# A two-layer fp32 encoder on one core: value weights loaded in layer 1's last phase, own buffers for raw weights, the last gated outputs kept on chip

## The chip, the cores and the metric

The kernel runs on one core of one Trainium2 chip. The metric is the device time of one execution in microseconds (us); the median of three runs of the kernel before is 2820.6 us (2820.55 to 2821.27). Engines are named as in the profile: PE is the matrix engine, PEld its loading of the stationary operand, DVE the vector engine, ACT the scalar engine, POOL GpSimd, and SP the engine whose queue issues all DMAs here, in one fixed order.

## The reference

The input x has 2048 tokens of 1024 channels. Layer 1 is a gated MLP mixer, layer 2 banded attention over the present and the eight previous chunks of 64 tokens, with 16 heads of 64 channels, a relative bias and a SiLU gate. Keys and values are projected from the residual stream after layer 1.

```python
h = rms_norm(x, a_norm_g);  x = x + gmlp_mixer(h, ...)         # layer 1
k, v = split(rms_norm(x, g_kv) @ w_kv)                         # shared keys, values
q, z = split(rms_norm(x, b_norm_g) @ w_qz)                     # layer 2
o = softmax(q * scale @ k.T + bias, band of 9 chunks) @ v      # per head
x = x + (o * silu(z)) @ w_out
return rms_norm(x, final_norm_g)
```

All of it is float32. The kernel writes every float32 product as three matmuls of a high and a low half (`mm3`, L111): high by high, high by low, low by high. Each operand is therefore split first: ACT casts the high half (L190, L226, L257) and DVE subtracts it to get the low half (L191, L227, L258).

## The kernel before

Tokens are worked in four tiles of 512 (t = 0 to 3), heads in eight pairs (p = 0 to 7). A scheduler at build time reorders the instructions of each engine by readiness; the order of the program text, the sizes of the buffer rings and the waits of rings for their last readers bound what it can do. A ring is a tag with `bufs` places: a new tile must wait until the readers of the tile that had its place are done.

The stages, by their time in the profiled execution:

- **Layer 1**, 0 to 1346.9. Its last part is the output product `Po`, a Strassen product of seven phases from 1037.9 on. Beside it `v_sums` prepares the value weights of the seven phases and stores them in DRAM (`vwf`). `block(0, b)` transposes the normed x of tile 0 and splits it at once into `hh`/`hl`, the two halves of the transposed x (16 KB per partition each).
- **Value stage** `vp`, 1346.9 to 1538.5. Per tile 14 products (seven phases in the order 1, 7, 2, 6, 5, 4, 3, two column halves `jp`), each of 12 matmuls. In tile 0 `v_right` loads the weights of each phase from `vwf` into `st` (2 places) as it is reached, and splits them. The loop also norms and transposes the x of tile t+1: all four `norm` calls stand at the tile's start, the four `block` calls at its steps 20, 28, 36 and 44.
- **Attention**, tile by tile from 1538.5, 1838, 2150 and 2465. For each pair `ahead` yields, in small steps, the products of the next pair: q and k (`project`), the gate z (`gate`), each 24 matmuls (`pj`), and a share of the Strassen out product `bo` of the tile before (`SHARE`, 56 steps per tile). The pair loop takes these steps between the eight scores `s`, transposes of the probabilities `tp` (`flip`) and value products `pv` of the present pair; `per` 16 spreads them over all eight rounds.
- **Weights of `pj`** (`weights`, L189): a raw weight of 512 KB is loaded on SP (L198 for t > 0, L200 for t = 0, where POOL also scales it by a gain at L181 and it is stored again), cast by ACT (`wh_b`, L190) and reduced by DVE (`wl_b`, L191). Raw, high and low half all take places of the one ring `T` of 8, which `bo`'s weights use too (loaded in halves from `ows`, L219).
- **`o_sums`** (L1213): makes the Strassen sums of the out weights in four units, each of four loads, seven splits, four POOL operations and 14 stores to `ows`. They run in pairs 1 to 4 of tile 0.
- **Gated outputs** `og` (L1366): stored per pair to DRAM (`ogd`) and loaded again as the quarters `A` by `o_left`, with sums on POOL (L1393).
- **Tail**, 2752.5 to 2808.5: `bo` of tile 3, which has no attention beside it.
- **`finish`** (L1448 to L1461): the final norm of a finished block: for t < 3 the row `y` is loaded back from DRAM (ring `bx`, 2 places), scaled and stored.

Of the kernel before, what the change touches and what calls it, by code (L numbers as in the profile page):

```python
# [33 lines left out]
def trunk_kernel(  # L34
# [34 lines left out]
    }  # L69
    khd = [  # L70
# [74 lines left out]
    th0 = []  # L145

    def block(t, b):
# [8 lines left out]
        if t == 0 and b == 0:  # L156
            th0.extend(x_tiles(0))
        for h in range(2):
            ks = slice(h * 4, h * 4 + 4)
            nc.scalar.copy(x3[:, ks, :], half[h][:])  # L160
            if t == 0:
                oh = th0[0][:, ks, b * P : (b + 1) * P]
                nc.scalar.copy(oh, half[h][:])
                tv(th0[1][:, ks, b * P : (b + 1) * P], half[h][:], oh.bitcast(F32), op=sub)
        if t > 0:
            nc.sync.dma_start(xtd[t][b][:], xt[:])
# [19 lines left out]
    def t_tile(name):  # L186
        return sh.tile([P, 1024], F32, tag="T", name=name, bufs=8)
# [5 lines left out]
    def weights(t, p, c):  # L193
        name = f"b{t}_{p}_{c}"
        raw = t_tile(f"raw_{name}")
# [10 lines left out]
    def o_right(t):  # L206
        def right(ph):
            out = []
            for q in range(2):
                name = f"bo{t}_{ph}_{q}"  # L210
                if t + 1 == NT and ph in (2, 3):
                    raw = t_tile(f"raw_{name}")
                    w = [w_tile(f"w{i}_{name}") for i in "hl"]
                    nc.sync.dma_start(raw[:], wb_out[1, ph - 2, q])
# [8 lines left out]

    PHS = (1, 7, 2, 6, 5, 4, 3)

    def strassen(name, right, left, evict):  # L226
# [3 lines left out]

        def ready(i):
            if i < len(todo):
                ph, jp = todo[i]
                if jp == 0:
                    rts[ph] = right(ph)
                views[i] = left(ph, jp)

        ready(0)
        for i, (ph, jp) in enumerate(todo):
            ps = pmm.tile([P, 512], F32, tag="mm", name=f"{name}_{ph}_{jp}")  # L240
            vs = views.pop(i)
            for k in range(4):
                hi, lo = rts[ph][k // 2]
                c = slice((k % 2) * 512, (k % 2) * 512 + 512)
                mm3(ps[:], *vs[k], hi[:, c], lo[:, c], k == 0, k == 3)
                if k == 1:
                    ready(i + 1)
                if k < 3:
                    yield
# [3 lines left out]
    def split_s(pool, bufs, name, src):  # L253
# [5 lines left out]
        return [(hi[:, k, :], lo[:, k, :]) for k in range(4)]  # L259

    with ExitStack() as actx:
# [732 lines left out]
        for u in range(4):  # L994
            for f_, o in zip(v_sums(u), (0, 4, 5, 7, 9)):
                at(nin + 6 + 11 * u + o, f_)
# [11 lines left out]

        at(nin + 51, b_open)
# [19 lines left out]
    with ExitStack() as vctx:  # L1029
        vp = vctx.enter_context(tc.tile_pool(name="vp", bufs=1, reuse_waits="tile"))  # L1030
        vw = {
            (ph, q): [vp.tile([P, 1024], F32R, name=f"vw{i}{ph}_{q}") for i in "hl"]
            for ph in (1, 7, 5, 4, 3) for q in range(2)
        }

        def v_right(t):
            def right(ph):
                if t == 0:
                    for q in range(2):
                        if ph in (2, 6):  # L1040
                            vw[ph, q] = [w_tile(f"vw{i}{ph}_{q}") for i in "hl"]
                        raw = vp.tile([P, 1024], F32, tag="st", name=f"st{ph}_{q}", bufs=2)
# [5 lines left out]
        def v_left(t):  # L1048
# [3 lines left out]
            def left(ph, jp):  # L1052
                a11, a12, a21, a22 = (raw(jp, r, h) for r in range(2) for h in range(2))
                quad = {1: (0, 0), 2: (0, 1), 4: (1, 1)}.get(ph)
                if t == 0 and quad:
                    r, h = quad
                    c = slice((2 * jp + r) * P, (2 * jp + r + 1) * P)
                    out = [(a[:, c], b[:, c]) for a, b in xT[t][4 * h : 4 * h + 4]]
                else:
                    src = {1: a11, 7: a11, 2: a12, 6: a11, 5: a21, 4: a22, 3: a12}[ph]  # L1060
                    out = split_s(
                        vp, 6, f"v{t}_{ph}_{jp}", src.rearrange("p (k c) -> p k c", k=4)
                    )
# [61 lines left out]
        for t in range(NT):  # L1125
            if t + 1 < NT:
                for b in range(TB):
                    norm(t + 1, b, v_junk)
            for i, _ in enumerate(strassen(f"vp{t}", v_right(t), v_left(t), v_evict(t))):
                if t + 1 < NT and i in (20, 28, 36, 44):  # L1130
                    block(t + 1, (i - 20) // 8)
        pt4x.close()
        ptr.open(name="ptr", bufs=1, space=PSUM)

    with ExitStack() as bctx:
        cb = bctx.enter_context(tc.tile_pool(name="cb", bufs=1, reuse_waits="tile"))
        sb = bctx.enter_context(tc.tile_pool(name="sb", bufs=2, reuse_waits="tile"))
        pss = bctx.enter_context(tc.tile_pool(name="bss", bufs=1, space=PSUM))
# [74 lines left out]

        def o_sums(u):

            q, i = divmod(u, 2)
            cs = slice(i * 512, i * 512 + 512)
            w = {}
            for rc in ((0, 0), (0, 1), (1, 1), (1, 0)):
                w[rc] = c_tile(f"wo{u}_{rc[0]}{rc[1]}")  # L1220
                nc.sync.dma_start(w[rc][:], wb_out[rc[0], rc[1], q][:, cs])
            b11, b12, b21, b22 = (w[k][:] for k in ((0, 0), (0, 1), (1, 0), (1, 1)))

            def keep(ph, src):
                hi, lo = (half_tile("S", f"so{u}_{ph}{x_}", 6, F32R) for x_ in "hl")
                nc.scalar.copy(hi[:], src)
                tv(lo[:], src, hi[:].bitcast(F32), op=sub)
                for n, y_ in enumerate((hi, lo)):
                    nc.sync.dma_start(ows[ph, q][:, n, cs], y_[:].bitcast(F32))

            def first():
                keep(1, b11)
                tg(b11, b12, b11, op=sub)
                tg(b12, b22, b12, op=sub)

            def second():
                keep(3, b22)
                tg(b22, b22, b11, op=sub)

            def third():  # L1240
                keep(2, b21)
                tg(b21, b21, b22, op=sub)

# [398 lines left out]
```

## Time and profile before

| what | value |
|---|---|
| median of three runs | 2820.6 us |
| profiled execution | 2819.17 us, of it 2817.4 us span |
| PE busy in the span | 2673.3 us, 95% |
| DVE, ACT, POOL busy | 1955.1, 1322.6, 907.6 us |
| loads and stores | 732.42 MB, mean 260 GB/s |
| stages: `Po`; value; attention t = 0, 1, 2, 3; tail | 309.0; 191.6; 299.5, 312.0, 315.0, 287.5; 56.0 us |

Two numbers are to be read together: how long PE had nothing in it (length of a stretch less PE's busy time), and PEclk, the clock that the throttle granted while it worked, as a share of full speed. At full speed a 128x512 matmul starts every 0.227 us, in slow stretches every 0.427 us. A row "PE pj L114 <- DVE wl_b L191: 11.2, 20, 1.2" says that PE's matmul `pj` of line 114 waited 11.2 us in 20 waits, 1.2 us at the longest, and that what ended the waits was DVE's `wl_b` of line 191.

### The profile page before, as it was taken

To read this page: it belongs to the slowest core of one execution; us is meant where nothing else is said; L and a number is where in the kernel's file an instruction comes from. 1 tells how busy PE (TensorE), PEld (TensorE's weight loads), DVE (VectorE), ACT (ScalarE), POOL (GpSimd) and SP (SyncE) were. 2 spreads that over 40 slices of the span, in tenths; PEclk is the share of its full clock that TensorE was granted. 3 is DMA by queue.
4 is the path that set the end of the run, shared out by engine and by line. 5 is a ranking of instruction groups with operands and counts; after the bars stand their busy time and mean duration, and the time that the engine had idled before them with its cause. 6 is when DMAs were issued, how large, how long until landed. Compare 5 with 4: busy or idle time off the path is not lost. (4 is left out here: it accounts for less than half of the span.)

```text
span 2817.4 us, 38771 instructions
## 1 busy us (share of the span) xinstructions
PE 2673.3 (95%) x13216; PEld 2220.0 (79%) x13216; DVE 1955.1 (69%) x3091; ACT 1322.6 (47%) x2356; POOL 907.6 (32%) x903
## 2 busy tenths in 40 slices
PE   8999999999999999999799878999989999999997
PEld 7888888888888888888578656788778887788775
DVE  5665776667666777567577565777777777877775
ACT  5422243434434343433554544655555555565552
POOL 3512244251532322041243444323232222322234
PEclk9999999999999999999999898999999999999997
DMA  7898999989989689685646777666667665765676
GB/s 299 322 335 322 365 336 333 327 316 332 322 292 326 246 302 344 210 286 210 231 171 218 250 258 255 207 206 199 207 212 252 206 207 184 262 206 180 193 231 242
DMA packets 274421, 732.42 MB, mean 260 GB/s; under 512 B 29488, under 2 KB 62256, under 8 KB 274224
## 3 DMA queue, kind: packets, MB, share of 16 engines
q1 hardware_dynamic: 274224, 729.94, 75.0%
q8 instruction: 105, 1.72, 0.2%
q14 instruction: 92, 0.75, 0.1%
HBM read 540.03 MB, written 179.31 MB: 255 GB/s over the span
## 5 line engine op out<-in xcount | busy, mean ns | idle before, releaser
L112 PE MATMUL P<-T,S 128*128 128x512 f32 x1248 | 495.7, 397 | 2.1 <-ACT S L311 2.1
L114 PE MATMUL P<-T,S 128*128 128x512 f32 x1248 | 489.8, 392 | 0.0
L113 PE MATMUL P<-T,S 128*128 128x512 f32 x1248 | 488.4, 391 | 1.1 <-DVE T L314 1.1
L1299 POOL TENSOR_SCALAR pr<-pr,sl 128x640 f32<-128x640 f32 (+4 forms) x256 | 206.1, 806 | 603.0 <-DVE sl L1298 529.8
L112 PE MATMUL pj<-hh_b,wh_b 128*128 128x512 f32 x768 | 318.3, 414 | 20.9 <-ACT wh_b L190 20.2
L114 PE MATMUL pj<-hh_b,wl_b 128*128 128x512 f32 x768 | 312.6, 407 | 14.2 <-DVE wl_b L191 13.9
L113 PE MATMUL pj<-hl_b,wh_b 128*128 128x512 f32 x768 | 307.8, 401 | 0.0
L114 PEld LDWEIGHTS P<-T,S 128*128 128x128 f32 x1248 | 234.9, 188 | 50.5
L112 PEld LDWEIGHTS P<-T,S 128*128 128x128 f32 x1248 | 235.5, 189 | 47.0 <-ACT S L311 2.3
L113 PEld LDWEIGHTS P<-T,S 128*128 128x128 f32 x1248 | 235.4, 189 | 46.7 <-DVE T L314 1.3
L1295 ACT ACTIVATE pr<-pr,nm 128x640 f32<-128x640 f32 (+4 forms) x256 | 195.0, 762 | 147.9 <-DVE nm L1288 147.0
L1323 DVE TENSOR_TENSOR pt<-tp,pt 128x640 fp32r<-128x640 f32 (+4 forms) x256 | 188.3, 736 | 61.5 <-ACT pt L1322 59.8
L1288 DVE CUSTOM_DVE_ANT_0 pr<-s,bias 128x640 f32<-128x640 f32 (+4 forms) x256 | 188.4, 736 | 50.4 <-PE s L1280 40.8
L1319 PE MATMUL tp<-ident,pr 128*128 128x128 f32 x1120 | 168.7, 276 | 33.7 <-DVE pt L1323 29.1
L1319 PEld LDWEIGHTS tp<-ident,pr 128*128 128x128 f32 x1120 | 133.8, 141 | 77.2 <-issue 32.2
L114 PEld LDWEIGHTS pj<-hh_b,wl_b 128*128 128x128 f32 x768 | 148.3, 193 | 56.4 <-DVE wl_b L191 25.5
L1322 ACT CAST pt<-tp 128x640 fp32r<-128x640 f32 (+4 forms) x256 | 158.2, 618 | 68.5 <-PE tp L1319 66.1
L112 PEld LDWEIGHTS pj<-hh_b,wh_b 128*128 128x128 f32 x768 | 148.7, 194 | 47.5 <-ACT wh_b L190 26.2
L113 PEld LDWEIGHTS pj<-hl_b,wh_b 128*128 128x128 f32 x768 | 148.9, 194 | 18.9
L191 DVE TENSOR_TENSOR wl_b<-raw_b,wh_b 128x1024 fp32r<-128x1024 f32 x96 | 130.7, 1361 | 46.1 <-ACT wh_b L190 40.1
L1347 PE MATMUL pv<-pt,V 128*128 128x256 f32 x960 | 152.2, 294 | 2.0 <-ACT pt L1322 2.0
L190 ACT CAST wh_b<-raw_b 128x1024 fp32r<-128x1024 f32 x96 | 100.7, 1049 | 111.1 <-DMA raw_b<-wk 57.6
(282 smaller groups left out, 5974.7 us busy)
## 6 DMA issues: line engine op xcount, KB each, us to landing
S<-hsd SPq DMA_DIRECT2D x288, 512.0 KB, 5.5
rw<-in_w_a SPq DMA_DIRECT2D x108, 512.0 KB, 6.4
A<-ytd SPq DMA_DIRECT2D x72, 512.0 KB, 5.7
raw_b<-wk SPq DMA_DIRECT2D x72, 512.0 KB, 4.2
hsd<-S SPq DMA_DIRECT2D x56, 512.0 KB, 4.5
V<-vhd SPq DMA_DIRECT2D x56, 512.0 KB, 4.7
wh_bo<-ows SPq DMA_DIRECT2D x52, 512.0 KB, 4.0
wl_bo<-ows SPq DMA_DIRECT2D x52, 512.0 KB, 4.9
```

The lines of the kernel that those rows point to most:

```text
L112: mm(ps, lh, rh, start=first, stop=False)
L113: mm(ps, lh, rl, start=False, stop=False)
L114: mm(ps, ll, rh, start=False, stop=last)
L190: nc.scalar.copy(wh[:], raw[:])
L191: tv(wl[:], raw[:], wh[:].bitcast(F32), op=sub)
L1288: nc.vector.tensor_tensor_reduce(out=pr[:, c0:].rearrange("p (a b) -> p a b", a=nseg), in0=ps[:, :nseg, :w], in1=bias[:, c0:].rearrange("p ...
L1295: nc.scalar.activation(pr[:, c0:], pr[:, c0:], AF.Exp, scale=-1.0, bias=nm[:], accum_out=sl[:])
L1299: nc.gpsimd.tensor_scalar(pr[:, c0:], pr[:, c0:], sl[:], 1.0, op0=ALU.mult, op1=ALU.mult)
L1319: tpose(tp[:, b, :], pr[:, b * P : (b + 1) * P], ident[:])
L1322: nc.scalar.copy(oh, tp[:, b0:5, :])
L1323: nc.vector.tensor_tensor(pt[:, 1, b0 + qq : 5 + qq, cs], tp[:, b0:5, :], oh.bitcast(F32), op=ALU.subtract)
L1347: mm(po[:, 0, :], keys(i), pt[:, j, i, :], start=(t == 0 and j == 0 and i == blocks[0]), stop=(j == 1 and i == blocks[-1]),)
```

## The change

1. **Value weights early.** `v_early` loads the raw weights of value phases 1 and 7 at step 46 of layer 1's output product and splits them at steps 48 and 49, into the places `hh` and `hl`. For that `block(0)` no longer writes the split x of tile 0 there; it is stored like the other tiles' x (`xtd`) and loaded and split by `reload(0)` at step 20 of value tile 3. Value tile 0 now splits all its left operands itself (6 splits more). The `v_sums` events stand 9 steps apart instead of 11. `weigh` lets the weights of phases run ahead (`look`), and `st` has 4 places, `S` in the value stage 8 instead of 6.
2. **Norms spread.** The four `norm` calls for tile t+1 stand at steps 1, 4, 7 and 10 of value tile t.
3. **Places for raw weights.** `raw_w` gives them a ring of their own: `raw` (4) for t = 0, `wr` (2) for t > 0. `T` then holds only halves: four weights at a time.
4. **`o_sums` moved and shortened.** Units 0 and 1 run in value tiles 1 and 2, units 2 and 3 in pairs 2 and 4 of tile 0. Phase 5's sum is stored raw as well (`owf`), and the last `bo` loads it raw and splits it, as it does with phases 2 and 3.
5. **Steps dealt differently.** `SHARE` for t < 3 is (2, 8, 8, 9, 9, 8, 8, 4), the last pair of a tile uses `per` 11, tile 0 counts no `bo` steps, and the first four steps of all are taken before the first score.
6. **Last gated outputs on chip.** For t = 3 pairs 0 to 5 of `ogd` are loaded during the last pair into `hh`/`hl` (`last_open`); pairs 6 and 7 are written there by DVE (`last_og`), and the sums are made per piece on POOL (`last_sums`). The ring `S` of layer 2 has 4 places instead of 6, `y` one place instead of 2.

```diff
+    def v_early(q, ph):
...
+        raw = sh.tile([P, 1024], F32, tag="raw", name=f"rv_{ph}_{q}", bufs=4)
+        nc.sync.dma_start(raw[:], vwf[ph, q][:])
+        return lambda: split_in(raw, *vw[ph, q])
...
+        at(nin + 46, early)
+        for i in range(4):
+            at(nin + 48 + i // 2, lambda i=i: splits[i]())
...
-            if t + 1 < NT:
-                for b in range(TB):
-                    norm(t + 1, b, v_junk)
+                if t + 1 < NT and i in (1, 4, 7, 10):
+                    norm(t + 1, i // 3, v_junk)
...
+                if t + 1 == NT and i == 20:
+                    reload(0)
+                if 0 < t < NT - 1 and i > 4 and i % 6 == 0 and todo:
+                    todo.pop(0)()
...
-    def t_tile(name):
-        return sh.tile([P, 1024], F32, tag="T", name=name, bufs=8)
+    def raw_w(t, name):
+        if t:
+            return raws[0].tile([P, 1024], F32, tag="wr", name=name, bufs=2)
+        return sh.tile([P, 1024], F32, tag="raw", name=name, bufs=4)
...
+            if hd == 1 and t + 1 == NT and p >= 6:
+                last_og(p, og32, zt[t, p])
...
+        def last_sums(cs):
+            x_ = {n: a[:, cs] for n, a in la.items()}
+            tg(x_["s1"], x_["10"], x_["11"], op=add)
+            tg(x_["s2"], x_["11"], x_["s3"], op=sub)
+            tg(x_["s4"], x_["01"], x_["s2"], op=sub)
...
-        SHARE = (2, 7, 7, 7, 7, 7, 7, 12)
+        SHARE = {t: (2, 8, 8, 9, 9, 8, 8, 4) for t in range(NT)}
+        SHARE[NT - 1] = (2, 7, 7, 7, 7, 7, 7, 12)
...
-                if t == 0 and 1 <= p <= 4:
-                    todo = o_sums(p - 1)
+                per = 11 if p + 1 == NPAIR and t + 1 < NT else 16
+                if t == 0 and p in (2, 4):
...
-                    y = sb.tile([P, 2, 512], F32, tag="bx", name=f"y{t}_{b}", bufs=2)
+                    y = sb.tile([P, 2, 512], F32, tag="bx", name=f"y{t}_{b}", bufs=1)
```

**PE at the step from layer 1 to the value stage.** Before: `tr_b<-bx_b` are the transposes of tile 0's last block, `tr_b<-xo_b` those of tile 1, `vp_1_0` and `vp_1_1` the first two value products.

```order
L114 MATMUL Po_7_11871<-To_30_11421,So_7_1_11747 128x512
L154 MATMUL tr_b_3_0_11899<-ident,bx_b_3_11819 128x128 x4
L154 MATMUL tr_b_3_1_11900<-ident,bx_b_3_11819 128x128 x4
L154 MATMUL tr_b_0_0_12102<-ident,xo_b_0_11941 128x128 x4
L154 MATMUL tr_b_0_1_12103<-ident,xo_b_0_11941 128x128 x4
L154 MATMUL tr_b_1_0_12171<-ident,xo_b_1_11949 128x128 x4
L154 MATMUL tr_b_1_1_12172<-ident,xo_b_1_11949 128x128 x4
L154 MATMUL tr_b_2_0_12237<-ident,xo_b_2_11957 128x128 x4
L154 MATMUL tr_b_2_1_12238<-ident,xo_b_2_11957 128x128 x4
L154 MATMUL tr_b_3_0_12300<-ident,xo_b_3_11965 128x128 x4
L112 MATMUL vp_1_0_11983<-vwh_0_11921,hh_b_11760 128x512
L112 MATMUL vp_1_1_12000<-vwh_0_11921,hh_b_11760 128x512
```

After the change, at the same place:

```order
L115 MATMUL Po_7_11880<-To_30_11431,So_7_1_11767 128x512
L153 MATMUL tr_b_3_0_11908<-ident,bx_b_3_11831 128x128 x4
L153 MATMUL tr_b_3_1_11909<-ident,bx_b_3_11831 128x128 x4
L113 MATMUL vp_1_0_11945<-vw_11474,Shv_1_0_11939 128x512
L114 MATMUL vp_1_0_11945<-vw_11474,Shv_1_0_11939 128x512
L113 MATMUL vp_1_1_11982<-vw_11474,Shv_1_1_11960 128x512
L115 MATMUL vp_1_0_11945<-vw_11474,Slv_1_0_11940 128x512
```

The eight groups of tile 1's transposes no longer stand ahead of the first value product; and that product reads an x split as every other tile's (`Shv`).

**ACT in a pair of tile 1.** `pr` is an exponential, `pt` a copy of transposed probabilities, `ot` a copy of a value product, `wh_b_6_1` and `wh_b_6_0` the casts of the weights of q and k for pair 6. Before:

```order
L1322 CAST pt_9_1_18288<-tp_9_3_18347 128x5x128
L1322 CAST pt_10_0_18398<-tp_10_0_18399 128x5x128
L1295 ACTIVATE pr_10_2_18381,sl_10_2_18383<-pr_10_2_18381,nm_10_2_18382 128x640
L257 CAST Sho_4_0_19099<-A_11_17536 128x512
L190 CAST wh_b_6_1_18389<-raw_b_6_1_18388 128x1024
L1295 ACTIVATE pr_10_3_18437,sl_10_3_18439<-pr_10_3_18437,nm_10_3_18438 128x640
L1322 CAST pt_10_0_18398<-tp_10_1_18450 128x5x128
L1359 COPY ot_9_1_18418<-pv_9_1_18407 64x512
L190 CAST wh_b_6_0_18492<-raw_b_6_0_18491 128x1024
L1295 ACTIVATE pr_11_0_18469,sl_11_0_18471<-pr_11_0_18469,nm_11_0_18470 128x640
```

After the change:

```order
L1317 ACTIVATE pr_10_0_18320,sl_10_0_18322<-pr_10_0_18320,nm_10_0_18321 128x640
L1344 CAST pt_9_1_18339<-tp_9_2_18340 128x5x128
L1381 COPY ot_9_0_18359<-pv_9_0_18348 64x512
L186 CAST wh_b_6_1_18457<-raw_b_6_1_18456 128x1024
L269 CAST Sho_5_1_18419<-A_10_16765 128x512
L186 CAST wh_b_6_0_18560<-raw_b_6_0_18559 128x1024
L1317 ACTIVATE pr_10_1_18392,sl_10_1_18394<-pr_10_1_18392,nm_10_1_18393 128x640
L1344 CAST pt_9_1_18339<-tp_9_3_18408 128x5x128
L269 CAST Sho_4_0_18769<-A_11_17548 128x512
L1498 ACTIVATE jk_110_18434,ssq_1_18433<-oc_110_18429 128x512
L1344 CAST pt_10_0_18469<-tp_10_0_18470 128x5x128
L1317 ACTIVATE pr_10_2_18449,sl_10_2_18451<-pr_10_2_18449,nm_10_2_18450 128x640
```

The two casts stand in the same pair, but ahead of exponentials and copies that they followed before (`pr_10_1` to `pr_10_3`, `pt_10_0`).

**SP around the start of the tail.** `y` is a row loaded for the final norm of tile 2, `out` its store, `wl_bo` and `wh_bo` weight halves of `bo`, `ogd` the stores of gated outputs, `A` their loads. Before:

```order
L219 DMA wl_bo_7_0_26168<-ows_0_114 128x1024
L1461 DMA out<-y_0_26038 128x512 x2
L1454 DMA y_2_26116<-x2d_2_174 128x1024
L219 DMA wh_bo_7_1_26171<-ows_1_115 128x1024
L1376 DMA ogd_163<-og_7_26108 128x2x128 x2
L1461 DMA out<-y_2_26116 128x512 x2
L219 DMA wl_bo_7_1_26172<-ows_1_115 128x1024
L214 DMA raw_bo_2_0_26213<-in_wb_out 128x1024
L1387 DMA A_01_26225<-ogd_163 128x1024
L1387 DMA A_11_26227<-ogd_163 128x1024
```

After the change:

```order
L1518 DMA y_3_25995<-x2d_3_177 128x1024
L1502 DMA x2d_0_174<-ou_1_0_23733 128x512
L1502 DMA x2d_2_176<-ou_1_1_23784 128x512
L215 DMA wh_bo_7_0_26182<-ows_0_114 128x1024
L1525 DMA out<-y_3_25995 128x512 x2
L215 DMA wl_bo_7_0_26183<-ows_0_114 128x1024
L215 DMA wh_bo_7_1_26186<-ows_1_115 128x1024
L1518 DMA y_0_26078<-x2d_0_174 128x1024
L215 DMA wl_bo_7_1_26187<-ows_1_115 128x1024
L1483 DMA row_26402<-x1d_63 128x512
L210 DMA raw_bo_5_0_26334<-owf_116 128x1024
L1525 DMA out<-y_0_26078 128x512 x2
```

The stores of `ogd` and loads of `A` are gone from this place; `wl_bo_7_1` now stands behind a load of `y` whose only place the store `out<-y_3` must have left.

More of the change, by code (lines that the diff above doesn't have):

```diff
@@ L69, in trunk_kernel @@
     }
+    owf = [dram.tile([P, 1024], F32, name=f"owf{q}") for q in range(2)]
     khd = [
@@ L194, in weights @@
         name = f"b{t}_{p}_{c}"
[L195 removed]
+        raw = raw_w(t, f"raw_{name}")
         w = w_tile(f"wh_{name}"), w_tile(f"wl_{name}")
@@ L1007, in block0, with early @@
                 norm(0, b + 2, acc_tile)
+        def early():
+            splits.extend(v_early(q, ph) for ph in (1, 7) for q in range(2))
+        splits = []
+        at(nin + 46, early)
+        for i in range(4):
+            at(nin + 48 + i // 2, lambda i=i: splits[i]())
         at(nin + 51, b_open)
@@ L1212, in gate @@
             zt[t, p] = z
[L1214 to L1242, printed above, removed]
-            return [first, second, third] + [
-                lambda ph=ph, o=o: keep(ph, o)
-                for ph, o in ((5, b11), (7, b12), (6, b22), (4, b21))
-            ]
         ogt = {}
@@ L1544, in trunk_kernel @@
         for u in range(2):
+            take(first, 4)
             score(0, 0, u)
-            take(first, 4)
         before = None
```

156 lines of the change are left out of this document (111 added, 45 removed).

## The prediction

> **What bounds the kernel now.** First the page, for the span, PE's load and the chain of waits that ended last.
>
> ```profile
> span 2817.4 us, 38771 instructions
> PE 2673.3 (95%) x13216; PEld 2220.0 (79%) x13216; DVE 1955.1 (69%) x3091; ACT 1322.6 (47%) x2356; POOL 907.6 (32%) x903
> ...
> PEclk9999999999999999999999898999999999999997
> ...
> PE 26%; DMA 8%; DVE 6%; ACT 3%; issue 2%; POOL 2%; SPq 1%; DVEq 0%; POOLq 0%; ACTq 0%
> ```
>
> PE is busy 95% of the span and its clock dips only in the second half. The chain names PE first, with pieces of DMA and DVE between. So PE bounds, and what can be won is where PE stands empty or works at a low clock. The second view is therefore the busy time by stage (length, then PE, PEld, DVE, ACT and POOL busy, PEclk, DMA share, GB/s).
>
> ```profile
> 1037.90:1346.90 309.00, 309.00 (x1384) 256.04 (x1383) 214.16 (x256) 114.64 (x181) 75.04 (x50) 1.00 0.73 258
> 1346.90:1364.90 18.00, 7.05 (x37) 6.47 (x36) 9.14 (x15) 11.51 (x21) 10.53 (x10) 0.62 0.57 219
> 1364.90:1412.90 48.00, 42.85 (x175) 31.03 (x174) 32.42 (x48) 29.06 (x48) 4.64 (x5) 1.00 0.79 267
> 1412.90:1538.50 125.60, 122.76 (x569) 100.77 (x568) 91.15 (x138) 62.22 (x127) 53.48 (x39) 1.00 0.54 186
> 1538.50:1838.00 299.50, 250.04 (x1171) 198.56 (x1170) 190.30 (x428) 155.55 (x346) 125.12 (x175) 0.90 0.74 245
> 1838.00:2150.00 312.00, 296.52 (x1646) 251.78 (x1645) 236.03 (x434) 181.30 (x326) 90.02 (x118) 0.98 0.67 213
> 2150.00:2465.00 315.00, 297.31 (x1633) 251.44 (x1632) 236.63 (x436) 181.13 (x325) 88.97 (x118) 0.97 0.67 215
> 2465.00:2752.50 287.50, 274.35 (x1547) 233.70 (x1546) 217.79 (x410) 165.96 (x303) 83.67 (x111) 0.99 0.64 204
> 2752.50:2808.50 56.00, 44.94 (x158) 33.29 (x157) 33.35 (x39) 17.22 (x32) 27.52 (x18) 0.82 0.72 259
> ```
>
> I call a stage's **loss** its empty time plus busy time times (1 - PEclk). Layer 1's last part has none: PE 309.00 of 309.00. Boundary: 10.95 + 7.05 x 0.38 = 13.6 us. First value tile 5.2, the other three 2.8. Attention t = 0: 49.5 + 25.0 = 74.5; t = 1: 15.5 + 5.9 = 21.4; t = 2: 17.7 + 8.9 = 26.6; t = 3: 13.2 + 2.7 = 15.9. Tail: 11.1 + 8.1 = 19.2. In all 179 us; the change touches every one of these stages, and PE's work stays the same apart from a few transposes that change place. The third view is the same table for tile 0, pair by pair.
>
> ```profile
> 1538.50:1579.50 41.00, 35.47 (x162) 29.28 (x161) 18.94 (x48) 17.48 (x38) 10.59 (x20) 0.92 0.81 259
> 1579.50:1615.90 36.40, 29.11 (x142) 23.12 (x140) 24.91 (x63) 20.14 (x48) 20.29 (x25) 0.88 0.76 245
> 1615.90:1653.80 37.90, 30.46 (x140) 23.83 (x140) 26.19 (x57) 20.51 (x49) 19.63 (x25) 0.93 0.81 274
> 1653.80:1694.80 41.00, 29.62 (x131) 22.67 (x131) 24.07 (x50) 18.51 (x42) 18.77 (x22) 0.88 0.76 253
> 1694.80:1737.50 42.70, 32.29 (x137) 24.24 (x137) 25.89 (x60) 20.89 (x49) 19.30 (x25) 0.83 0.76 250
> 1737.50:1762.50 25.00, 23.54 (x110) 18.99 (x111) 12.86 (x26) 10.61 (x23) 9.20 (x14) 0.94 0.80 259
> 1762.50:1787.20 24.70, 23.93 (x125) 19.35 (x125) 15.64 (x42) 13.72 (x33) 11.05 (x18) 1.00 0.65 215
> 1787.20:1853.60 66.40, 61.21 (x320) 50.72 (x319) 52.01 (x109) 42.93 (x87) 19.19 (x33) 0.92 0.68 222
> ```
>
> Rows 2 to 5 are the pairs that carry `o_sums`; their losses are 10.8, 9.6, 14.9 and 15.9 (mean 12.8). Rows 6 and 7 do without: 2.9 and 0.8 (mean 1.8). A unit of `o_sums` thus goes with 11.0 us, of which 3.0 are clock (mean 3.7 less 0.7).
>
> **Term A, the boundary: -12 us.**
>
> ```profile
> 1358.83 6.33 PE L154 MATMUL tr_b<-ident,xo_b 128*128 128x128 f32 x28 [10.94 <-DVE rr_b L125]
> ```
>
> PE stood still 10.94 us for the norm of tile 1, whose transposes lie ahead of the first value product. In the new order that product follows tile 0's last transposes directly; its left operand comes from blocks 0 and 1, which are long done, and its weights are split in layer 1. What is late next is at most a cast and a subtraction of a left operand, about 1.5 us. So 12 of 13.6 go; I bound it by 10 and 13.6. The four loads and splits moved into `Po` lie beside a PE that is full, where ACT is busy 114.64 and DVE 214.16 of 309 us; if one came late, it would cost about 1.2 us each.
>
> **Term B, the first value tile: -2.5 us.** Two phases' weights are there already and `st` loads two phases ahead: half of 5.2, bounds 0 and 5. Six splits more, and the reload of x for tile 0 (four loads, four casts, four subtractions) cost nothing: in the later value tiles PE is full (122.76 of 125.60) while DVE has 34 and ACT 63 us free. If that cover went, six splits would be 6 x 0.7 = 4 us.
>
> **Term C, two units of `o_sums` in value tiles 1 and 2: +4 us.** No row shows them there. From one side they cost nothing, in the same cover; from the other as much as in attention, 11.0 each. I take 2 each, nearer to the row of the value tiles: a product of 12 matmuls lasts 12 x 0.23 = 2.7 us there, and its split takes DVE 0.68 (second row below).
>
> ```profile
> L1233 POOL TENSOR_TENSOR wo<-wo,wo x4: 1270/1282/1290, 1580.6 to 1702.6; 128x512 f32<-128x512 f32 x4
> L258 DVE TENSOR_TENSOR Slv<-xo_b,Shv x28: 676/684/2127, 1412.1 to 1533.4; 128x512 fp32r<-128x512 f32 x28
> ```
>
> (Shortest, median and longest in ns.) A subtraction of 684 ns took up to 2127 ns. [...]
>
> **Term D, attention of tile 0: -36.5 us.** Two units gone: 2 x 11.0 = -22. The other two stand in pairs 2 and 4 with a pair free between them and with weight loads that no longer share `T`: a quarter of 2 x 11.0, -5.5. The opening loses 5.5 + 35.47 x 0.08 = 8.4 us (first row), in which weights are loaded behind the value stage's stores on SP; three raw weights can now be ahead: -5. The last row loses 5.2 + 4.9 = 10.1; the steps of the last pair are dealt faster: -4. Bounds: 22 less 11 for steps dealt worse, so 11, and 60 (all 74.5 but 1.8 for each of eight pairs).
>
> **Term E, tiles 1 to 3: -13 us.**
>
> ```profile
> PE pj L114 <- DVE wl_b L191: 11.2, 20, 1.2
> PE pj L112 <- ACT wh_b L190: 8.1, 7, 1.8
> ACT wh_b L190 <- DMA raw_b<-wk: 57.3, 35, 6.2
> SPq L198 <- PE pj L114: 67.0, 24, 8.9
> ```
>
> These are waits between 1840 and 2740. PE waits 11.2 + 8.1 = 19.3 us for split weights; ACT waited 57.3 us for raw weights to land; and SP could not issue their loads for 67.0 us, because a place of `T` is free only when PE has read it. With their own ring the loads no longer wait for PE. The empty time of the three tiles is 46.3 and the clock's part 17.6, so 19.3 us of waits carry 19.3 x 1.38 = 26.6. I take half, -13: the cast now waits itself for a place of `T`, and the ACT rows show the two casts only a few instructions ahead of before. Bounds 0 and 27.
>
> **Term F, the tail: -9 us.**
>
> ```profile
> 2757.92 0.39 PE L113 MATMUL bo<-wl_bo,Sho 128*128 128x512 f32 x1
> 2758.15 0.39 PE L114 MATMUL bo<-wh_bo,Slo 128*128 128x512 f32 x1
> ...
> 2762.28 0.79 PE L113 MATMUL bo<-wl_bo,Sho 128*128 128x512 f32 x1 [3.52 <-DMA wl_bo<-ows]
> 2762.87 0.63 PE L114 MATMUL bo<-wh_bo,Slo 128*128 128x512 f32 x1
> 2763.30 0.63 PE L112 MATMUL bo<-wh_bo,Sho 128*128 128x512 f32 x1
> ...
> 2774.43 0.71 PE L112 MATMUL bo<-wh_bo,Sho 128*128 128x512 f32 x2
> ```
>
> ```profile
> 2755.59 0.88 SPq L1376 DMA_DIRECT2D ogd<-og  x2
> 2756.57 0.92 SPq L1461 DMA_DIRECT2D out<-y  x2
> 2757.58 0.40 SPq L219 DMA_DIRECT2D wl_bo<-ows  x1
> ```
>
> A weight stood behind the last `ogd` stores on SP; PE waited 3.52 us for it and then started a matmul each 0.43 us instead of 0.23 until 2774.4: 12.1 us x (1 - 0.23/0.43) = 5.6. Together 9.2. After, no `ogd` store is there, and no sums wait for a reload. Against it: phase 5 is now split raw as well, POOL makes its sums amid the last pair's work, and `y` has one place, so a load waits for a store ahead of `wl_bo` on SP. Bounds 0 and 17 (19.2 less the loss of a free pair).
>
> **Sum.** -12 - 2.5 + 4 - 36.5 - 13 - 9 = -69 us. The profiled execution took 2819.2 us (2817.4 and 1.8 around the span), 1.4 less than the median of the runs. 2819.2 - 69 = 2750.2, as a median **2751 us**.
>
> **The rivals.** (1) **`o_sums` costs the same in the value stage**: C is +22 instead of +4, 2769 us. For it, DVE is the busiest helper there (73%); against it, the value tiles keep PE 98% full with ACT half idle. (2) **The raw load was not the bound**: the places of the halves in `T` are as few as before for PE's purposes, E is 0 and D loses its -5.5 and -5: 2774 us. For it the ACT rows, which hardly move; against it 57.3 us of ACT's waiting on loads. (3) **Short gaps do not slow the clock**, so that only long ones give clock time back: the clock's part of D and E, 27% of 49.5 = 13 us, stays: 2764 us.
>
> ```profile
> PE pj L112 <- ACT wh_b L190: 12.1, 8, 3.1
> ```
>
> Against it, this wait of tile 0 is 3.1 us at its longest, and its pairs still show 0.83 to 0.93. [...] (4) **The tail doesn't do what it says**, the one place of `y` or the sums on POOL eating the gain: F is 0, 2760 us. (5) **All losses fall to the level of a free pair**: A -13.6, B -5, C 0, D -60, E -27, F -17: 2698 us. (6) **Slower: the wait of the weights moves from SP's queue to ACT's.** A raw weight no longer waits for PE, but its cast does, and ACT works in order: behind the waiting cast stand the exponentials and the copies of `tp` and `ot` that PE's next `tp` and `pv` need. Its price: SP's 67.0 us in 24 waits come to stand on ACT and reach PE with clock, 67.0 x 1.38 = 92, in place of E's -13: 2751 + 13 + 92 = 2856 us. It makes the whole slower from (69 - 13)/1.38 = 41 us of such waits on. For it, the ACT rows: the casts now stand before `pr_10_1` to `pr_10_3`. Against it, `T` now holds four weights, not two and two thirds, so the place asked for was read longer ago.
>
> **How the numbers follow.** Forecast 50%, (1) 12%, (2) 12%, (3) 4%, (4) 7%, (5) 4%, (6) 11%. The range 2700 to 2798 takes in the forecast with its bounds, since they do not all fall on one side, and (1) to (4); (5) and (6) lie outside, 15%, and 5% of the others. A measurement can tell 0.2%, 5.6 us, from no change: below 2815 is faster. Of (6) a price of 37 to 45 us of waits falls within, 2%, the rest is slower, 9%: faster 0.89, same 0.02, slower 0.09.
>
> **What would show it.** A: no wait of PE over 2 us at the end of layer 1. B, C: the first value tile near 45 us, all four near 175 (173.6 before). D: tile 0 near 263 us, its free pairs under 26. E: waits of PE for `wl_b` and `wh_b` under 10 us in tiles 1 to 3, and SP's wait for PE at the load of raw weights gone. F: the tail near 47 us without a gap over 2 us. Wrong would make it above all waits of ACT's `wh_b` for PE of more than 40 us (6), or pairs of tile 0 that stay near 37 us without their `o_sums` (the cause of the loss is another).

## The result, and the profile after

The changed kernel took 2734.2 us in the median of four runs (2731.5 to 2742.3), the kernel before 2820.9: a ratio of 0.969 (95% interval 0.967 to 0.972). That is 87 us less where 69 were forecast, inside the stated range. That the total fell inside the range is in part luck, because two errors of opposite sign met in it: the boundary and the value stage together took 9.5 us more where 10.5 less were forecast, and attention of tiles 1 to 3 gave 34 us more than its term.

The page of the profiled execution after the change: span, engines, clock, chain of waits.

```profile
span 2729.7 us, 38869 instructions
PE 2629.2 (96%) x13216; PEld 2199.6 (81%) x13216; DVE 1970.0 (72%) x3097; ACT 1327.0 (49%) x2360; POOL 907.7 (33%) x906
...
PEclk9999999999999999999989999999999999999999
...
PE 30%; DVE 6%; DMA 4%; ACT 2%; issue 2%; POOL 1%; SPq 0%; DVEq 0%; POOLq 0%; ACTq 0%
```

PE runs as many matmuls as before, but its busy time fell from 2673.3 to 2629.2 us, and DMA's part of the chain from 8% to 4%. By stage (length, then PE, PEld, DVE, ACT, POOL, PEclk, DMA share, GB/s), from the end of layer 1 on:

```profile
1347.50:1350.00 2.50, 1.27 (x10) 0.93 (x8) 0.69 (x2) 1.62 (x4) 0.00 (x0) 1.00 0.21 80
1350.00:1404.00 54.00, 46.21 (x200) 37.50 (x201) 44.43 (x60) 34.52 (x62) 24.39 (x19) 0.91 0.73 260
1404.00:1452.40 48.40, 43.83 (x201) 35.78 (x200) 34.01 (x55) 26.14 (x55) 20.46 (x17) 0.96 0.80 271
1452.40:1502.20 49.80, 43.48 (x202) 34.42 (x201) 38.28 (x58) 26.48 (x55) 23.36 (x19) 1.00 0.77 259
1502.20:1549.00 46.80, 41.17 (x170) 33.56 (x169) 39.75 (x48) 21.35 (x39) 21.37 (x12) 0.93 0.66 227
1549.00:1823.00 274.00, 248.88 (x1266) 202.79 (x1265) 192.62 (x433) 159.53 (x350) 108.78 (x171) 0.96 0.79 254
1823.00:2121.00 298.00, 289.24 (x1641) 249.39 (x1640) 236.73 (x438) 183.15 (x326) 91.32 (x118) 0.98 0.70 227
2121.00:2415.00 294.00, 287.56 (x1641) 247.73 (x1641) 237.91 (x439) 182.80 (x327) 90.91 (x118) 0.99 0.72 232
2415.00:2673.00 258.00, 251.47 (x1451) 216.32 (x1450) 204.00 (x382) 153.83 (x285) 83.39 (x110) 1.00 0.63 200
2673.00:2721.00 48.00, 39.77 (x155) 28.82 (x154) 35.49 (x44) 18.66 (x34) 21.52 (x15) 0.96 0.74 253
```

To compare the two traces I cut both at the same events: the first matmul of each value tile, each tile's first gate activation `Z`, the last product of the value stage, the last value product `pv` of attention. "The end" is PE's last matmul. Then:

| stretch | before | after | change | forecast |
|---|---|---|---|---|
| end of layer 1 to first value product | 18.3 | 2.5 | -15.8 | A -12 |
| value tile 0 | 47.9 | 54.0 | +6.1 | B -2.5 |
| value tiles 1 and 2 | 86.5 | 98.2 | +11.7 | C +4 |
| value tile 3 | 39.1 | 46.6 | +7.5 | 0 |
| end of the value stage to tile 1's first gate | 315.3 | 274.1 | -41.2 | D -36.5 |
| from there to tile 3's last gate | 857.3 | 810.6 | -46.7 | E -13 |
| last `pv` to the end | 56.2 | 48.1 | -8.1 | F -9 |

(The rest is +0.9 us in layer 1 and -1.8 between the last gate and the last `pv`.) Tile 0 from its second gate to its seventh, cut at the gates:

```profile
1598.90:1626.80 27.90, 25.44 (x129) 21.02 (x130) 21.29 (x49) 16.78 (x41) 12.23 (x22) 0.94 0.83 264
1626.80:1656.80 30.00, 26.89 (x134) 21.59 (x133) 21.49 (x47) 16.96 (x39) 14.74 (x20) 0.94 0.78 245
1656.80:1684.70 27.90, 24.87 (x134) 20.23 (x133) 21.37 (x49) 17.19 (x40) 15.53 (x22) 1.00 0.88 288
1684.70:1715.50 30.80, 26.55 (x134) 21.59 (x134) 20.94 (x46) 16.86 (x39) 14.01 (x20) 0.94 0.76 238
1715.50:1741.20 25.70, 25.17 (x134) 20.32 (x133) 19.40 (x48) 15.83 (x37) 13.08 (x20) 1.00 0.86 287
```

The two units of `o_sums` do not lie in rows 2 and 4, as their places in the program text (pairs 2 and 4) suggest: DVE makes their low halves from 1592.7 to 1621.3 and from 1651.1 to 1686.3, for the most part in rows 1 and 3, and these rows are no longer than rows 2 and 4. So what a unit costs in its own pair can't be read off. As an estimate, the first four rows together are 13.8 us longer than four times the fifth (25.7), about 7 us a unit; by the same measure it was 14.7 before (36.4, 37.9, 41.0 and 42.7 against 24.8).

### The profile page after: what moved, and what is told of

Same layout as the page of the kernel before. It is cut to its first block, busy times and chain, and to the rows that moved or that the text cites. A ratio compares the mean times of both kernels' runs of the same rounds, so it can differ in the third digit from the quotient of the medians.

```text
span 2729.7 us, 38869 instructions
## 1 busy us (share of the span) xinstructions
PE 2629.2 (96%) x13216; PEld 2199.6 (81%) x13216; DVE 1970.0 (72%) x3097; ACT 1327.0 (49%) x2360; POOL 907.7 (33%) x906
## 5 line engine op out<-in xcount | busy, mean ns | idle before, releaser
L115 PE MATMUL pj<-hh_b,wl_b 128*128 128x512 f32 x768 | 305.6, 398 | 0.0
L114 PEld LDWEIGHTS P<-T,S 128*128 128x128 f32 x1248 | 235.2, 188 | 46.6 <-DVE T L363 1.3
L113 PEld LDWEIGHTS pj<-hh_b,wh_b 128*128 128x128 f32 x768 | 147.5, 192 | 25.7 <-ACT wh_b L186 5.8
L1369 PE MATMUL pv<-pt,V 128*128 128x256 f32 x960 | 142.4, 288 | 0.9 <-ACT pt L1344 0.9
L1369 PEld LDWEIGHTS pv<-pt,V 128*128 128x128 f32 x960 | 127.0, 193 | 3.1 <-ACT pt L1344 1.8
```

Of the source, the lines that this page charges most:

```text
L113: mm(ps, lh, rh, start=first, stop=False)
L114: mm(ps, lh, rl, start=False, stop=False)
L115: mm(ps, ll, rh, start=False, stop=last)
L1369: mm(po[:, 0, :], keys(i), pt[:, j, i, :], start=(t == 0 and j == 0 and i == blocks[0]), stop=(j == 1 and i == blocks[-1]),)
```

## The experiments

All are edits of the changed kernel unless said otherwise.

**e1, raw weights back in the ring `T`.**

```diff
-        if t:
-            return raws[0].tile([P, 1024], F32, tag="wr", name=name, bufs=2)
-        return sh.tile([P, 1024], F32, tag="raw", name=name, bufs=4)
+        return sh.tile([P, 1024], F32, tag="T", name=name, bufs=8)
```

> The changed kernel, only with the raw weights of attention back in the ring T (part 3 undone). From the first gate of tile 1 to the last of tile 3 the kernel before took 857.2 us and the changed one 810.6, 46.6 less, where the prediction had 13. Theory (own places for raw weights give nearly all of it, since SP's loads no longer wait for PE): this stretch comes back to 840 or more, PE's waits for wl_b and wh_b there to 15 to 25 us (4.2 in the changed kernel, 19.3 before), the time to 2765 to 2780. Rival (the new dealing of steps gives it): the stretch stays below 822 and the time at 2734 to 2745.

Measured: 2777.4 us (2773.1 to 2781.6), the stretch of tiles 1 to 3 840.9 us. PE's and ACT's waits in that stretch, and SP's at the loads of raw weights (L192, after the change L194), of e1:

```profile
ACT wh_b L184 <- DMA raw_b<-wk: 42.6, 30, 5.0
PEld pj L115 <- DVE wl_b L185: 19.6, 32, 1.9
PE pj L115 <- DVE wl_b L185: 12.0, 19, 1.5
PE tp L1339 <- DVE pt L1343: 11.8, 18, 1.8
PE pj L113 <- ACT wh_b L184: 5.1, 4, 2.0
SPq L192 <- PE pj L115: 51.5, 20, 8.9
```

and of the changed kernel:

```profile
PE tp L1341 <- DVE pt L1345: 6.9, 10, 2.4
PE pj L113 <- ACT wh_b L186: 4.2, 3, 2.0
ACT wh_b L186 <- PE pj L114: 4.6, 4, 1.8
ACT wh_b L186 <- PE bo L114: 3.8, 4, 1.1
ACT wh_b L186 <- issue: 9.8, 6, 1.8
SPq L194 <- DVE sl L1320: 115.2, 25, 7.9
SPq L194 <- DVE wl_b L187: 63.4, 14, 8.6
```

With the own places ACT's waits for the load (42.6 us) and PE's for `wl_b`, at the matmul and at its weight load, are gone. SP still waits at the raw loads, but for DVE, which reads the raw weights, and no longer for PE. The casts wait for PE 8.4 us in all, at most 18.2 with the 9.8 us for whose end the profile names nothing. With the raw weights in `T` the waits come back, and the tail also grows to 60.5 us, where three phases of the last `bo` are split raw: splits of `bo`'s weights end 9.8 of the 16.5 us that PE stands empty there. The theory holds: 30 of the 46.7 us hang on this part alone.

**e5, own places alone**, in the kernel before: the same `raw_w`, with `S` 4 and `y` 1 for room.

> The kernel before with own places for raw weights alone (with the smaller rings that make room for them: S 4, y 1). Putting the raw weights back into T cost the changed kernel 43 us, 30 of them in tiles 1 to 3. Theory (the places are worth this by themselves): tiles 1 to 3 fall from 857 to 820 to 832, the time to 2775 to 2790. Rival (they need the new dealing of steps or the missing o_sums): tiles 1 to 3 stay above 842, the time above 2800.

Measured: 2766.8 us (2764.3 to 2768.6), ratio 0.980 (0.978 to 0.981); tiles 1 to 3 took 813.8 us, tile 0 to the first gate 302.0. So this part alone brings 43.5 of the 46.7 us, against the theory's 25 to 37, and 13 us of D; together more than half of the whole gain. (The smaller rings `S` and `y` are in it.)

**e2, the old dealing of steps** (`SHARE`, `per`, the count for tile 0, the first four steps).

```diff
-        SHARE = {t: (2, 8, 8, 9, 9, 8, 8, 4) for t in range(NT)}
+        SHARE = {t: (2, 7, 7, 7, 7, 7, 7, 12) for t in range(NT)}
...
-                per = 11 if p + 1 == NPAIR and t + 1 < NT else 16
+                per = 16
...
```

> The changed kernel with the old dealing of steps (SHARE, 16 instead of 11 in a tile's last pair, the count for tile 0, the first four steps behind the first score). Theory (raw places): only the crossings from tile to tile get longer, about 3 us each and a few us in tile 0: 2740 to 2750, the stretch of tiles 1 to 3 at 815 to 825 us. Rival (the dealing gives the gain): the stretch at 840 or more, 2765 to 2780.

Measured: 2739.8 us (2739.4 to 2741.9), ratio 0.970 (0.968 to 0.973); tiles 1 to 3 took 818.9 us, tile 0 to the first gate 271.3. In the time the intervals overlap with the changed kernel's, so the gain of 6 us is not shown there. In tiles 1 to 3 the dealing is worth some 8 us, as the theory said: the kernels below that keep it and the raw places took 805.9 to 811.5 us. Tile 0 did not get longer without it, against the theory.

**e3, all four units of `o_sums` in attention.**

```diff
-                if t == 0 and p in (2, 4):
-                    todo = o_sums(p // 2 + 1, lambda n: half_tile("C", n, 4), lambda n: half_tile(
+                if t == 0 and 1 <= p <= 4:
+                    todo = o_sums(p - 1, lambda n: half_tile("C", n, 4), lambda n: half_tile(
...
```

> The changed kernel with all four units of o_sums in pairs 1 to 4 of attention tile 0, as before the change. Theory (they cost less beside the value products): value tiles 1 and 2, now 48.4 and 49.8 us, fall to about 44 and 42, tile 0 grows by 2 x 11 us, so 2734 + 22 - 12 = 2744. Rival (a unit costs the same wherever it stands): value tiles and tile 0 trade evenly, 2729 to 2739. Third (with raw places a unit costs attention little): tile 0 grows by less than 8 us and the time falls below 2732.

Measured: 2752.4 us (2749.2 to 2755.3). Value tiles 1 and 2 fell to 41.7 and 41.9 us, with PE full; tile 0 grew by 36 us, to 310.1:

```profile
1407.40:1449.10 41.70, 41.70 (x202) 34.83 (x201) 29.96 (x51) 25.13 (x54) 16.48 (x15) 1.00 0.63 213
1449.10:1491.00 41.90, 41.90 (x202) 34.72 (x201) 32.54 (x50) 21.02 (x46) 17.48 (x14) 1.00 0.61 204
```

A unit costs 7.3 us beside the value products (14.6 for two), and the two that came back to attention cost 18 each, now that four stand in a row. The theory's direction holds, both its sizes were too small.

**e6 and e6b, why a unit costs 7 us in the value stage.** e6 makes the units' sums on DVE there; e6b gives their stored halves a ring of their own.

```diff
+        tg = nc.vector.tensor_tensor if u < 2 else nc.gpsimd.tensor_tensor
...
-                        [P, 512], F32R, tag="S", name=n, bufs=8
+                        [P, 512], F32R, tag="so", name=n, bufs=4
```

> The changed kernel with the eight POOL sums of the two o_sums units of the value stage done by DVE. Without these units value tiles 1 and 2 took 41.7 and 41.9 us, with them 48.4 and 49.8. Theory (POOL operations hold up DVE's subtractions, and that costs the 14.6 us): the tiles fall to 43 to 45 each, 2722 to 2727. Rival (the halves of o_sums share the ring S with the left operands, and a place is free only when its store has left): the tiles stay at 48 to 51, 2732 to 2740.

> The changed kernel with a ring of four places of their own for the halves that o_sums stores in the value stage. Theory of the ring: ACT's casts of left operands no longer wait for stores (7.7 us in 2 waits in the changed kernel), value tiles 1 and 2 fall to 42 to 45 each, 2720 to 2727. Theory of POOL beside DVE: the tiles stay at 47 to 50, 2732 to 2738.

Measured: e6 2727.9 us (2723.5 to 2733.7), tiles 47.8 and 46.3; e6b 2728.8 us (2725.2 to 2731.1), tiles 41.7 and 46.7. In the changed kernel the value stage shows

```profile
PE vp L115 <- DVE Slv L270: 16.3, 5, 5.6
ACT Shv L269 <- DMA ows<-so_1h: 7.7, 2, 4.3
PE vp L113 <- ACT Shv L269: 6.7, 4, 3.4
```

and e6, in tiles 1 and 2, still

```profile
PE vp L113 <- ACT Shv L269: 5.4, 2, 2.9
ACT Shv L269 <- DMA ows<-so_1h: 4.3, 2, 3.6
```

while in e6b no cast of a left operand waits for a store. The ring is all of tile 1's loss; in tile 2 either edit takes back some 3 of 8 us. Neither theory is the whole; the ring has the larger part, and what keeps tile 2 at 45.5 us even with both (e10, below) stays open. All this is read from the tiles: the times of both kernels (ratio 0.966, 0.965 to 0.968) overlap with the changed kernel's.

**e4 and e9, what removed the boundary.** e4 puts the four norms ahead of the value tile again (the first two parts of the edit below); e9 loads and splits the weights of phases 1 and 7 in the value stage (the last two).

```diff
+            if t + 1 < NT:
+                for b in range(TB):
+                    norm(t + 1, b, v_junk)
...
-                if t + 1 < NT and i in (1, 4, 7, 10):
-                    norm(t + 1, i // 3, v_junk)
...
-        at(nin + 46, early)
...
-                if t == 0 and ph not in (1, 7):
+                if t == 0:
...
```

> The changed kernel with the four norms of tile t+1 ahead of value tile t again (part 2 undone). Theory (term A comes from the norms' place): a wait of PE of 8 to 11 us for a norm stands again between layer 1 and the first value product, and the first value tile gets shorter by no more than 3: 2740 to 2745. Rival (the early weights alone give term A, and the spread norms only load DVE later): no such wait, the first value tile falls from 54.0 to about 50, 2728 to 2734.

> The changed kernel with the weights of value phases 1 and 7 loaded and split in the value stage, into the same places. The norms' place made no difference (2733.5). Theory (the early weights alone removed the boundary): the first value product starts 12 to 18 us after layer 1's last product instead of 2.5, the first value tile keeps its 54, 2742 to 2750. Rival (the x of tile 0 split in the value stage, or the shorter v_sums, did it): it starts within 5 us, 2730 to 2738.

Measured: e4 2733.5 us (2728.5 to 2734.4), first value product 2.5 us after layer 1. e9 2732.8 us (2729.9 to 2733.5), first value product after 9.6 us, value tile 0 49.6 us. The start of e4, and the first product's wait of e9:

```profile
1351.82 1.04 PE L153 MATMUL tr_b<-ident,bx_b 128*128 128x128 f32 x8
1354.10 0.50 PE L113 MATMUL vp<-vw,Shv 128*128 128x512 f32 x1 [1.24 <-ACT Shv L269]
```

```profile
1358.23 1.22 PE L113 MATMUL vp<-vw,Shv 128*128 128x512 f32 x2 [8.30 <-ACT vw L186]
```

With early weights the norms' place in the program does nothing; the rival of e4 holds for the gap, though value tile 0 took 54.4 us in it, not 50. But e4's norms did not run ahead of the first product: ACT begins them at 1360.2, 6 us behind it. Late weights bring back 7 us of gap, less than e9's theory asked, and most of it returns in tile 0 (59.2 us to the end of that tile, 56.5 changed, 66.2 before); no difference is left in the time. What gives the other 7 us against before (the spread norms, tile 0's own splits, four places of `st`, the wider `S`) was not tried apart.

**e7, the first gains on DVE.**

```diff
-            scaled(raw, (bg if c else kg)[:, :, :])
+            scaled(raw, (bg if c else kg)[:, :, :], nc.vector if p == 0 or (p == 1 and c == 1) else None)
```

> The changed kernel with the gain of the first four raw weights of attention applied by DVE instead of POOL; in the changed kernel POOL does it during value tile 3, which takes 46.6 us (39.1 before, 38.7 with the raw weights in T, where these operations start later). Theory (POOL's three operations of 2.1 us without a pause hold up DVE, whose two short subtractions took 4.15 us there, and PE waits 5.6 us): value tile 3 falls to 39 to 42, 2727 to 2731, though DVE gets 4 x 1.2 us more to do. Rival (DVE is full there from the reload of x): value tile 3 stays at 46 or grows to 50, 2734 to 2740.

Measured: 2730.5 us (2726.9 to 2731.3), value tile 3 42.0 us. DVE and POOL of the changed kernel in that tile:

```profile
1517.34 1.22 DVE L168 TENSOR_TENSOR hl_b<-xr_b,hh_b 128x1024 fp32r<-128x1024 f32 x1
1518.47 4.15 DVE L1136 TENSOR_TENSOR v<-vc,v 128x256 fp32r<-128x256 f32 x2
1522.55 2.38 DVE L270 TENSOR_TENSOR Slv<-xo_b,Shv 128x512 fp32r<-128x512 f32 x1
```

```profile
1518.24 2.07 POOL L173 TENSOR_TENSOR raw_b<-raw_b,bg 128x1024 f32<-128x1024 f32 x1 [5.96 <-DMA raw_b<-in_w_kqz]
1520.31 2.04 POOL L173 TENSOR_TENSOR raw_b<-raw_b,kg 128x1024 f32<-128x1024 f32 x1
1522.31 2.07 POOL L173 TENSOR_TENSOR raw_b<-raw_b,bg 128x1024 f32<-128x1024 f32 x1
```

Two subtractions that take 0.75 us elsewhere took 4.15, the next 2.38 instead of 0.68, exactly beside POOL's three gains, and PE waited 5.6 us for that last one. With the gains on DVE, which then has about as much to do in less time (39.09 of 42.0 us), the tile is 4.6 us shorter:

```profile
1504.80:1546.80 42.00, 39.58 (x169) 31.01 (x168) 39.09 (x52) 21.17 (x39) 17.59 (x10) 1.00 0.78 265
```

The theory fits this place, but the gain is not shown. Seven other kernels with the gains on POOL (e2, e3, e4, e6, e6b, e8, e9) took 43.7 to 48.3 us in this tile, e10 and e11 with them on DVE 46.6 and 44.5. What e7 saves in the tile it loses behind it (280.5 us to tile 1's first gate, 274.1 changed), and its time (ratio 0.967, 0.965 to 0.968) overlaps with the changed kernel's.

In e1, where the reload of x stands in the same tile but only two gains run in it, from 1530.2 on, the tile took 38.7 us: the reload alone is free. The early gains alone are free too. e5 has no reload, and POOL makes seven gains in this tile, from 1505.2 on; DVE was stretched there by 12.9 us, and PE stayed full:

```profile
1502.80:1541.50 38.70, 38.64 (x170) 31.52 (x169) 35.30 (x38) 17.31 (x32) 28.84 (x15) 1.00 0.69 234
```

Only the kernels with both lost the 5 to 9 us: the own places sent the gains forward to right behind the reload, whose four subtractions (1.22 us each) DVE had just finished. As e5 is made from the kernel before, it differs in more than this; the two were not parted within one kernel.

**e8, gated outputs through DRAM again.**

```diff
-            if hd == 1 and t + 1 == NT and p >= 6:
-                last_og(p, og32, zt[t, p])
-            elif hd == 1:
+            if hd == 1:
...
```

> The changed kernel with the last gated outputs stored and loaded again as before (last_og, last_open and their sums undone; rings and phase 5 as changed). From the last value product to the end: 56.2 us before, 48.1 changed, 58.9 with own raw places alone, 60.5 with the raw weights in T. Theory (the stay on chip gives the tail's gain): 56 to 60 us, 2742 to 2747. Rival (the missing wait for a weight behind the ogd stores came from the order on SP, or from the raw places): 50 us or less, 2731 to 2738.

Measured: 2743.9 us (2742.5 to 2744.6), 59.9 us from the last `pv`. PE's three largest gaps in its tail:

```profile
2684.77 0.50 PE L113 MATMUL bo<-wh_bo,Sho 128*128 128x512 f32 x1 [2.55 <-ACT Sho L269]
2697.35 0.80 PE L113 MATMUL bo<-wh_bo,Sho 128*128 128x512 f32 x1 [2.04 <-ACT Sho L269]
2722.66 1.22 PE L113 MATMUL bo<-wh_bo,Sho 128*128 128x512 f32 x2 [3.92 <-ACT wh_bo L186]
```

The stay on chip is worth 12 us of tail here and 10 of the time, so the theory holds. PE's empty time in the tail is 15.7 us, 8.2 in the changed kernel. Left operands end 8.7 us of it (4.5 changed), splits of raw weights 7.0 (1.8 changed): without the stay on chip both come late. No wait for a loaded weight over 0.1 us is among them, though the `ogd` stores are back on SP. In the changed kernel the largest gap left is one:

```profile
2677.39 0.50 PE L114 MATMUL bo<-wl_bo,Sho 128*128 128x512 f32 x1 [1.86 <-DMA wl_bo<-ows]
```

**e10 and e11, a faster version.** e10 joins e6, e6b and e7; e11 adds one phase of look-ahead instead of two in value tile 0.

```diff
-                strassen(f"vp{t}", v_right(t), v_left(t), v_evict(t), 1 if t else 2)
+                strassen(f"vp{t}", v_right(t), v_left(t), v_evict(t), 1)
```

> The changed kernel with an own ring for the halves of o_sums in the value stage, their sums on DVE there, and the first four gains on DVE. Theory (ring and POOL each cost their part): value tiles 1 to 3 at 42 to 44, 42 to 44 and 39 to 42 instead of 48.4, 49.8 and 46.6, 2712 to 2722. Rival (DVE is the bound of these tiles and takes the place of POOL): tiles at 45 to 48, 2725 to 2732.

> The kernel of e10 (own ring, sums and first gains on DVE) with the weights of value tile 0 loaded and split one phase ahead instead of two. In the changed kernel ten splits of 1.22 us each stand close together on DVE in that tile, and PE waits 5.5 us for a left operand's subtraction behind them; with phases 1 and 7 late the tile took 49.6 us instead of 54.0. Theory (the bunched splits cost the tile): value tile 0 falls from 54.5 to 48 to 51, the time from 2722.6 to 2717 to 2720. Rival (the splits have to be made anyway and now come late for their own products): tile 0 stays at 54 or grows, 2722 to 2726.

Measured: e10 2722.6 us (2715.5 to 2725.6), ratio to before 0.964 (0.962 to 0.965), value tiles 1 to 3 41.7, 45.5 and 46.6; e11 2721.5 us (2714.4 to 2723.0), ratio 0.963 (0.961 to 0.965), value tile 0 51.1 us, tiles 1 to 3 43.5, 46.9 and 44.5. Both beat the changed kernel (0.967 to 0.972). Tile by tile both theories are half right. In e10's tile 3 DVE is busy 45.20 of 46.70 us, the rival's case:

```profile
1492.10:1538.80 46.70, 41.65 (x169) 31.95 (x168) 45.20 (x57) 23.94 (x45) 18.28 (x10) 0.96 0.74 251
```

e11's tile 0 is 3.4 us shorter than e10's, at the edge of what its theory asked; the time differs by 1.1 us, less than either kernel's spread, so against e10 no gain is shown.

## Why the prediction was right or wrong

**A, -12: right in size, the cause only half named.** The gap shrank by 15.8 us. "PE stood still 10.94 us for the norm of tile 1" reads the wait rightly, but it was not the only thing that held the first product. In the kernel before, ACT's first cast of the value weights ran at 1362.8 and DVE's splits began only at 1364.0, 0.9 us ahead of the first product:

```profile
1362.81 1.06 ACT L190 CAST vwh<-st 128x1024 fp32r<-128x1024 f32 x1
L191 DVE TENSOR_TENSOR vwl<-st,vwh x14: 1215/1224/1604, 1364.0 to 1409.5; 128x1024 fp32r<-128x1024 f32 x14
```

The raw weights had landed at 1357.3; the cast came 5.5 us later because on ACT it stood behind norm sums and copies of tile 1's transposes. So the norms held the product in two ways, and without them the weights' own load would have held it until 1358 at least. The runs agree: with spread norms and late weights the gap is 9.6 of 18.3 us (e9), with early weights 2.5 whatever the norms' place in the program (e4). Late weights behind norms were not tried in the changed kernel. A wait names what ended it, not what PE would have waited for next.

**B, -2.5: wrong, +6.1.** The step that failed is "half of 5.2": loading ahead moved splits of 1.22 us close together, seven of the tile's ten into the 15 us from 1370.4 on; one left operand came 5.5 us late behind them, and the granted clock in the tile was 0.91. e9, with weights late, gives the tile 49.6 us, and e11, which looks one phase ahead, 51.1 against e10's 54.5. A and B together gave -9.7 for -14.5.

**C, +4: wrong, +11.7 against before, 14.6 for two units by e3.** "I take 2 each" failed: I bounded by engines' free time, while the units put their stored halves into the ring of the left operands (e6b). Rival (1) is what happened in the value stage: 7.3 of the 11 per unit.

**The reload "costs nothing": right by itself (e1), wrong beside the moved gains:** +7.5 in value tile 3. The gains were not in the sum at all. The prediction counted the three raw weights ahead as a gain of D's opening, and did not ask what POOL then does earlier, right behind the reload (e5 has the gains without it, at no cost).

**D, -36.5: right in sum, -41.2**, with its parts only partly separated, so that the agreement may be chance: 13 come with the raw places alone (e5), 36 is what two more units cost there (e3), where 22 were taken. The opening, put at -5, gave nothing up to the first gate (40.8 us before, 42.1 after) and 2 up to the second.

**E, -13: mechanism right, size wrong.** Between the cuts PE's empty time fell from 41.2 to 17.1 us, and its busy time times (1 - PEclk) from 14.6 to 8.4. There is a third part. Counting each matmul from its start to the next against the usual pitch of its kind in these traces (0.227 us for 512 columns, 0.145 for 320, 0.118 for 256, 0.109 for 128), the stretch lost 88 us before and 43 after: 32 and 17 us of it lie under PE's busy time. Of the 46.7 us thus some 24 are empty time, 6 clock and 15 slower pace. The step that failed is "I take half" of 26.6: PE's waits for `wl_b` and `wh_b` fell from 19.3 to 4.2 us, with the clock 21 us where 13 were taken. The rest was put at nothing. In the kernel before, the same stretch also has

```profile
PEld pj L114 <- DVE wl_b L191: 20.9, 47, 1.4
PE tp L1319 <- DVE pt L1323: 14.1, 18, 2.5
```

The first row, waits at the weight load, is gone after the change; 9.7 of the 20.9 us lay under PE's busy time and may be part of the 15 us of pace. The second fell to 6.9 us; that products were now at hand to fill between would explain it, but was not tried. The dealing of steps had no term in E either; it is worth 8 us in this stretch by e2, and by e5, which has the old dealing, at most 3. Rival (2) is refuted by e1 and e5. Rival (6) did not come: the casts' waits for PE are 8.4 us, at most 18.2, where 41 were needed.

**F, -9: right in size, -8.1, by luck.** The step that failed is "a weight stood behind the last `ogd` stores on SP". e8 has these stores back, and so has e5; neither shows a wait of PE in the tail for a loaded weight over 0.1 us, and still their tails are 59.9 and 58.9 us. What the stay on chip saves are waits for left operands and for splits of raw weights (e8), which were not priced; that the raw places matter as much there (60.5 us in e1) was not in it. Rival (4) is refuted.

**Rival (3)** does not hold here. In tiles 1 to 3 busy time times (1 - PEclk) fell, as said, from 14.6 to 8.4 us, though PE's longest wait there was 3.1 us before and 2.4 after. What the prediction says against it, a longest wait of 3.1 us in tile 0, is that of one row; another there, of `s` for `K`, reaches 5.5 us. But the clock was granted at one half also behind short gaps, in the kernel before for 6.8 us from 1590.2 on, where PE's longest gap in the 7 us ahead was 1.5 us.

## What to carry to other kernels

When raw and finished weights share a ring, the load waits for the consumer of an earlier finished one (in tiles 1 to 3 SP waited for PE 67.0 us before, 51.5 in e1); places of its own for the raw tile were worth 57 of the 87 us here (e5). Price a wait also at the weight load and as lost pace, not only as empty time of PE. And when something is let run earlier, follow each engine that it touches, and each ring that it borrows, to where it now lands: what was gained in attention was partly paid back in the value stage. Two moves that are each free can cost when they meet (e1, e5), so a move is to be tried with the others and without them.

## What the runs showed of the hardware

DVE instructions were stretched only beside POOL. From the end of layer 1 on, 73 DVE instructions before the change and 82 after it took over 0.3 us more than the lower quartile of those of the same line and shape, 57.8 and 72.9 us in all; every one of them overlaps a POOL instruction, though POOL is busy only 33% and 36% of that time. Of the 73, 72 read two operands in SBUF, of the 82, 80. Beside the three gains of the changed kernel's value tile 3 (2.07, 2.04 and 2.07 us without a pause), three DVE instructions in a row (2.12, 2.11 and 2.38 us) each ended 0.3 to 0.6 us behind one gain. What this costs depends on the slack: in e3's value tile 2 DVE was stretched by 7.7 us and PE stayed full (41.90 of 41.90), in e5's value tile 3 by 12.9 us with PE full, too; in value tile 3 of the changed kernel, which has the reload as well, 11.1 us of it went with a wait of PE of 5.6 us.
